# A planned kernel's order of instructions: a recorded list of 1677 search steps in place of 40 search rounds at build time

## The chip, the cores and the metric

The kernel runs on one core of one Trainium2 chip. The metric is the time of one execution in device microseconds. Before the change three runs were timed; their median stands below. One further execution was taken by the hardware profiler, and every view of the profile is of that one.

## The reference, cut to what matters

One inference step of a two-layer decoder in fp32, for a prompt of 512 tokens and a group of 8 x 8 sample tokens, which share all weights (576 tokens together; model width 1024, FFN width 2816):

```python
for i in range(DEPTH):                      # DEPTH = 2
    h = rms_norm(x, norm_mix_pre[i])
    if i % 2 == 0:
        m, nb = pool_mixer(h, ...)          # trailing means of 2, 4, 8, 16 tokens, a linear map per group
    else:
        m, nc, ns = gdn_mixer(h, ...)       # 8 q/k heads, 16 v heads of 128; chunked gated delta rule
    x = x + rms_norm(m, norm_mix_post[i])
    h = rms_norm(x, norm_ffn_pre[i])
    x = x + rms_norm(swiglu(h, ffn_w_in[i], ffn_w_out[i]), norm_ffn_post[i])
```

The outputs are x for both groups and the new states of the mixers.

## The kernel before, in words

Every product in fp32 accuracy is made from fp32r parts: an operand is split into a high and a low part (`wh`, `wl` for weights, `hH`, `hL` and `aH`, `aL` for activations), and `mm3` adds three matmuls per 128-row slice into one PSUM bank. ScalarE makes the high part, VectorE or GpSimd the low part. The 576 columns lie in two halves of 256 and 320 columns (`HALVES`); PSUM ring A of three banks serves the first half, ring B the second. In the DeltaNet layer other rings share the eight banks: `m` (two banks) for the projections, `s`, `k`, `x` and `g` for scan, inverse and transposes. Within the FFN a Strassen-like form (`seven`) is used. Weights arrive by SyncE's DMA queue in tiles of 128 x 1024 (`wraw`, three buffers) and are split as they come.

In time the work is: the pooling mixer, the first FFN, the projections and gates of the DeltaNet layer, its four groups of heads (`core`: inverse of the triangular matrices, scan over four chunks, sample heads) with the next group's projections, the output projection in two parts, and the second FFN. The first part of the output projection goes to DRAM (`y_d`); after the DeltaNet's tile pools are closed it is loaded again as `yo`, and the second part is added to it.

No engine's order is written by hand. The class `Plan` (from line 54) records every operation with its costs on each engine that may do it (`cost`), its predecessors, its shape mode on TensorE, and the PSUM tiles it holds. `finish` (line 267) then plans:

- `forward` (line 356) is a list scheduler. It walks through modelled time; on the engine that is free first it takes the ready operation with the highest `rank`. It models the DMA queue, the time of a change between TensorE's tile shapes, the TensorE clock by its load in a window, and the port that VectorE and GpSimd share. Operations marked for two engines (`EITHER`: VectorE or GpSimd; `BOTH`: VectorE or ScalarE) go to the one that takes them first. Where TensorE would wait over 300 ns in this model, `idle_until` puts dummy matmuls into an idle bank (`ps_w`, line 296; they compute nothing that is used). It returns the modelled length, the order and the times.
- `backward` (line 315) gives, for such an order, the latest time at which each operation could start. Its negative serves as the next rank.
- Before the change, `finish` made a first rank from the longest path, then 40 rounds: rank from `backward`, shifted per output tensor by a random amount of a width drawn from 0, 0, 300, 1000 and 3000 (modelled ns), then `forward`. A better round became the base of the next; the best of all was issued.

The instructions are issued in the order found, each engine's queue in strict order. All recorded operations therefore carry the line of that issue, L300, in the profile (dummies L296).

Of the kernel before, what the change touches and what calls it, by code (L numbers as in the profile page):

```python
# [4 lines left out]

# [45 lines left out]
ZB = (0, 4, 8, 10, 12, 16)  # L51


class Plan:


# [210 lines left out]
    def finish(self):  # L267
        self.on = False
        ops = self.ops
        n = len(ops)  # L270
# [4 lines left out]
        rank = [0.0] * n
        for i in range(n - 1, -1, -1):
            e = ops[i][7]
            hold, done = ops[i][1][e]
# [4 lines left out]
            rank[i] = r
        draw = random.Random(self.SEED)
        here = best = self.forward(rank)
        for _ in range(self.ROUNDS):
# [4 lines left out]
            if found[0] < best[0]:
                best = found
        with self.tc.manual_schedule():
            for i, e in best[1]:
                if e is None:
                    self.tc.nc.tensor.matmul(self.banks[i[0]][i[1]][0][:, :self.idle.shape[1]], self.idle, self.idle,  # L296
                                             start=True, stop=True)
# [2 lines left out]
                calls[e](*a, **k)  # L300

    def stirred(self, rank, stir, draw):

        if not stir:
            return rank
        off = {}
        for o in self.ops:
            off.setdefault(self.name(o), stir * (2.0 * draw.random() - 1.0))
        return [r + off[self.name(o)] for r, o in zip(rank, self.ops)]
# [506 lines left out]

# [1131 lines left out]
```

## Time and profile before

| what | value |
|---|---|
| median of 3 runs (lowest, highest) | 1572.15 us (1570.51, 1574.17) |
| the profiled execution's own time | 1572.64 us |
| its span, first to last instruction | 1570.9 us |
| instructions | 30641 |
| mean granted TensorE clock | 0.991 |
| HBM read, written | 166.65 MB, 30.52 MB |
| mean DMA rate over the span | 126 GB/s |

How to read it: PE is TensorE's matmuls, PEld its weight loads, DVE is VectorE, ACT ScalarE, POOL GpSimd, SP the SyncE queue that issues the DMAs. A row of a group gives the line, engine, operation, output<-inputs by tile name with the shape, the count, then the busy time in us and the mean ns of one, then the idle time just before. A row of the timeline gives the start and the length in us; in brackets stands the idle time before it and what ended that. In the windows view a row is one stretch: its length, then each engine's busy time with its count of instructions, the granted TensorE clock, the mean share of the DMA engines and GB/s. Matmuls are pipelined: several that overlap count once in the busy time.

### The profile page before, as it was taken

The page shows a single profiled execution, that of the slowest core. Times are in us where ns is not written, and L with a number is a line of the kernel's source. Part 1 is how long each engine was busy: PE and PEld are TensorE (multiplying, and loading weights), DVE is VectorE, ACT ScalarE, POOL GpSimd, SP SyncE. Part 2 cuts the span into 40 slices and gives each one's busy share as a digit, 9 for nine tenths or more (in the row PEclk, how much of TensorE's full clock was granted, in tenths as well). Part 3 has the DMA queues.
Part 4 walks back from the last instruction along what each step waited for, and adds up shares of the span by engine and source line. Part 5 has one row for each costly group of instructions (what it writes and reads, how often), then busy time and mean ns, then how long its engine had stood idle before and what let it go on. Part 6 is the DMA issues. An engine that isn't in the chain of part 4 may idle for free. (4 is left out here: it accounts for less than half of the span.)

```text
span 1570.9 us, 30641 instructions
## 1 busy us (share of the span) xinstructions
PE 1542.9 (98%) x11962; PEld 1481.2 (94%) x11962; DVE 1154.5 (73%) x2333; ACT 841.1 (54%) x1756; POOL 113.1 (7%) x258
## 2 busy tenths in 40 slices
...
PEclk8999999999999999999999999999999999999999
...
GB/s 184 103 178 142 82 94 95 96 80 91 151 210 158 83 119 117 102 123 100 136 109 108 106 127 120 201 140 179 248 173 177 107 81 73 88 110 68 98 187 119
DMA packets 350359, 198.92 MB, mean 127 GB/s; under 512 B 13963, under 2 KB 344364, under 8 KB 350207
## 3 DMA queue, kind: packets, MB, share of 16 engines
...
q14 instruction: 50, 0.41, 0.1%
HBM read 166.65 MB, written 30.52 MB: 126 GB/s over the span
## 5 line engine op out<-in xcount | busy, mean ns | idle before, releaser
L300 ACT ACTIVATE wh<-wraw 128x1024 fp32r<-128x1024 f32 (+1 forms) x227 | 233.5, 1032 | 263.2 <-PE ps_B L300 94.4
L300 DVE TENSOR_TENSOR wl<-wraw,wh 128x1024 fp32r<-128x1024 f32 (+2 forms) x226 | 268.0, 1191 | 113.6 <-ACT wh L300 74.9
L300 PE MATMUL ps_m<-hH,wh 128*128 128x320 f32 (+1 forms) x832 | 244.1, 310 | 2.7 <-ACT zz L300 2.6
L300 PE MATMUL ps_m<-hL,wh 128*128 128x320 f32 (+1 forms) x832 | 242.4, 306 | 0.0
L300 PE MATMUL ps_m<-hH,wl 128*128 128x320 f32 (+1 forms) x832 | 239.2, 306 | 0.0
L300 PEld LDWEIGHTS ps_m<-hH,wh 128*128 128x128 f32 x832 | 153.3, 189 | 7.6 <-ACT zz L300 3.6
L300 PEld LDWEIGHTS ps_m<-hL,wh 128*128 128x128 f32 x832 | 154.0, 190 | 2.3 <-issue 0.6
L300 PEld LDWEIGHTS ps_m<-hH,wl 128*128 128x128 f32 x832 | 152.6, 190 | 2.8 <-issue 0.8
L300 PE MATMUL ps_B<-hH,wh 128*128 128x320 f32 (+1 forms) x392 | 115.8, 306 | 0.2
L300 PE MATMUL ps_B<-hH,wl 128*128 128x320 f32 (+1 forms) x392 | 115.0, 305 | 0.0
L300 PE MATMUL ps_B<-hL,wh 128*128 128x320 f32 (+1 forms) x392 | 114.6, 304 | 0.0
L300 PE MATMUL ps_A<-hH,wh 128*128 128x256 f32 (+1 forms) x376 | 106.0, 293 | 2.8 <-DVE yo L300 1.9
L300 PE MATMUL ps_A<-hH,wl 128*128 128x256 f32 (+1 forms) x376 | 105.6, 292 | 0.5 <-DVE wl L300 0.5
L300 PE MATMUL ps_A<-hL,wh 128*128 128x256 f32 (+1 forms) x376 | 104.5, 290 | 0.1
L300 PE MATMUL ps_B<-aH,wl 128*128 128x320 f32 x352 | 103.5, 312 | 0.2 <-DVE wl L300 0.2
L300 PE MATMUL ps_B<-aH,wh 128*128 128x320 f32 x352 | 102.4, 311 | 0.0
L300 PE MATMUL ps_B<-aL,wh 128*128 128x320 f32 x352 | 101.9, 310 | 0.0
L300 PE MATMUL ps_A<-aH,wh 128*128 128x256 f32 x352 | 95.1, 283 | 0.4 <-ACT wh L300 0.4
L300 PE MATMUL ps_A<-aL,wh 128*128 128x256 f32 x352 | 94.0, 281 | 0.0
L300 PE MATMUL ps_A<-aH,wl 128*128 128x256 f32 x352 | 92.9, 282 | 0.0
L300 DVE SCALAR_TENSOR_TENSOR ac<-u,cwt,ac 128x600 f32<-128x600 f32 x96 | 80.9, 850 | 1.9 <-ACT ac L300 1.7
L300 ACT ACTIVATE aH<-sg 128x576 fp32r<-128x576 f32 (+2 forms) x56 | 32.3, 581 | 84.7 <-DVE sg L300 84.7
...
## 6 DMA issues: line engine op xcount, KB each, us to landing
...
```

The costliest lines, as they stand in the source:

```text
L300: calls[e](*a, **k)
```

## The change

`ROUNDS`, `STIR`, `SEED`, the random draws and `stirred` go. A string `MOVES` of 1677 entries comes, each of five numbers in base 36: `again.seed.stir.lo.hi`. `finish` starts from the same first rank and applies them in turn. An entry whose first field is 1 (16 of them, ten at the head of the list) replaces the rank by the backward pass of a forward pass. An entry with a width `stir` then adds to the rank of the operations lo to hi - 1 a noise of that width, which a hash makes from the seed and from the number of the first operation that writes the same tensor, so that operations that fill one tensor move together. The widths are 100 (550 entries), 300 (499), 1000 (363), 3000 (254) and 0 (11). Most ranges span 400, 100 or 1500 operations (573, 447 and 372 entries), a few the whole list; the highest bound is 15384. No order is compared with another any more: one last forward pass gives the order that is issued. `cost`, `forward`, `backward`, the operations and their data are unchanged.

```diff
+MOVES = """
+1.1eas61x.2s.4js.4mk 1.b5wlw6.2s.0.3q1 1.ktpsok.0.8pv.8sn 1.1ure0dv.0.5jj.6p7 1.hgmh6k.8c.981.bvc 1.7nyzhf.0.0.bvc
...
+"""
...
-    ROUNDS, STIR, SEED = 40, (0.0, 0.0, 300.0, 1000.0, 3000.0), 2
...
-        draw = random.Random(self.SEED)
-        here = best = self.forward(rank)
-        for _ in range(self.ROUNDS):
-            late = self.backward(here[1], here[2])
-            found = self.forward(self.stirred([-t for t in late], draw.choice(self.STIR), draw))
-            if found[0] < here[0] or draw.random() < 0.1:
-                here = found
-            if found[0] < best[0]:
-                best = found
+        first = {}
+        of = [first.setdefault(self.name(o), i) for i, o in enumerate(ops)]
+        for move in MOVES.split():
+            again, seed, stir, lo, hi = (int(x, 36) for x in move.split("."))
+            if again:
+                rank = [-t for t in self.backward(*self.forward(rank)[1:])]
+            if stir:
+                for i in range(lo, hi):
+                    rank[i] += stir * self.noise(seed, of[i])
+        best = self.forward(rank)
         with self.tc.manual_schedule():
...
+    @staticmethod
+    def noise(seed, who):
+
+        h = seed ^ (who * 2654435761 & 0xffffffff)
+        h ^= h >> 16
+        h = h * 0x85ebca6b & 0xffffffff
+        h ^= h >> 13
+        h = h * 0xc2b2ae35 & 0xffffffff
+        h ^= h >> 16
+        return h / 2147483648.0 - 1.0
```

More of the change, by code (lines that the diff above doesn't have):

```diff
@@ L2 @@
 import heapq
-import random
 from contextlib import ExitStack
@@ new lines @@
+0.yzlrz0.2s.0.s8 0.8bsca3.2s.2au.3gi 0.pd5qwx.8c.1zs.35g 0.1dkcr1g.2s.46o.49g 0.gohce9.8c.8hh.8k9
+0.1qmox10.2bc.7y1.895 0.1q0ubx9.8c.30w.3c0 0.2t46nq.8c.123.1d7 0.1f02old.2s.4cp.4nt 0.7uf57y.2s.383.3j7
+0.1io2edi.8c.6n2.6y6 0.d51t3g.8c.3ab.3lf 0.kyski6.2s.bg7.brb 0.nwmwau.8c.5ct.5fl 0.5q7dse.2bc.6gs.6jk
+0.94x3jt.2bc.52k.5do 0.173ehem.2s.3d.65 0.17dm05h.2s.1ar.2gf 0.7o5v0r.2s.a5c.bvc 0.19kwyb0.8c.5qe.5t6
+0.8fkj3m.2s.915.a6t 0.1gm8lpy.2s.4bn.5hb 0.gseya0.2bc.1jr.2pf 0.hb806i.rs.553.5g7 0.13th0bt.rs.bk1.bv5
@@ new lines @@
+0.xire0f.rs.1wy.32m 0.1wjfc1e.2s.9nf.at3 0.5mangj.rs.7re.7u6 0.1xbgl15.rs.7rh.82l 0.13tvkzy.rs.amh.axl
+0.ngzet1.rs.7wq.87u 0.1gjwecl.rs.2fc.2i4 0.xyipxv.8c.3ba.3me 0.12nn3ct.8c.2oc.3u0 0.3f9jym.2s.8d3.8fv
+0.ms49lm.8c.16t.2ch 0.10t15hv.8c.4zi.656 0.x1uzs9.2bc.9ni.9qa 0.1ipkmmg.2s.8oy.902 0.1du3687.rs.6vq.6yi
+0.7x2jcw.2s.aax.bgl 0.gu97up.8c.0.76 0.1hxvrax.8c.9q4.avs 0.y21u0p.2s.5fw.5r0 0.2bbt96.2bc.7ts.84w
+0.yldecn.2bc.11b.1cf 0.1tpg0gw.8c.1k3.1v7 0.rw51dw.8c.58h.6e5 0.8bcpst.rs.98t.aeh 0.7wpeg2.8c.8ql.91p
@@ new lines @@
+0.1y9p531.rs.3dl.3gd 0.m4xezo.8c.95k.ab8 0.1gj3768.2s.hn.1nb 0.51qq2b.2bc.2j6.2ly 0.1k3nqyr.2s.5lv.6rj
+0.y6ucev.rs.7z0.8a4 0.wxbkvk.2bc.7s3.837 0.1baxiw5.2s.0.kx 0.1q32nai.2s.70r.86f 0.1h4y1oy.2s.8jk.9p8
+0.1ttntui.8c.8c6.8na 0.1sdrihh.2bc.83k.86c 0.fun4eh.8c.bn5.bvc 0.1qmi15h.2s.0.t4 0.1o1of45.2s.618.76w
+0.1hdgjk2.rs.4mj.4pb 0.omnp9u.rs.6ox.6rp 0.1sta659.rs.5fw.5r0 0.fm47zb.8c.237.38v 0.v8iq9s.2s.73x.89l
+0.18l101a.2s.57e.92a 0.1ac1io.8c.7u7.8zv 0.1gvwjwn.2s.1xz.33n 0.1fxjl6j.2s.0.33f 0.5ez5wd.8c.3y8.49c
@@ new lines @@
+0.c9qi10.rs.azi.bam 0.ukl6ns.8c.7m6.7xa 0.141w03z.2s.9za.aae 0.4xpjy3.rs.7w2.876 0.wys13.2s.9u1.a55
+0.iwwn7d.8c.6xu.83i 0.hmfcbd.2bc.5cr.5fj 0.11wfrkv.rs.1fo.1qs 0.yc4sup.2s.77a.8cy 0.156z55c.rs.6p4.708
+0.wc5cgv.2s.6dr.6ov 0.kebtqw.8c.7be.7e6 0.1ui5xrl.2s.5p.40l 0.1kyvof3.8c.1hk.2n8 0.catp73.2bc.28f.2jj
+0.idq53h.8c.9j2.bvc 0.13d7t0r.8c.bbs.bmw 0.196fy4l.2s.2z4.44s 0.1jy9dbc.2s.6k1.6mt 0.hjty3u.2s.98l.ae9
+0.15bi1vd.8c.95m.bvc 0.1yyy23b.rs.1kd.1n5 0.167ecek.8c.9rt.a2x 0.idlzw1.2s.71u.awq 0.1sy5idv.rs.2i3.2kv
@@ new lines @@
+0.19s07wq.2bc.are.au6 0.5wbkzi.2s.8e3.9jr 0.30oiia.2bc.9hs.ang 0.ubjoux.2bc.96f.997 0.1idrsdh.2s.0.4f
+0.1345wfi.2bc.nw.z0 0.wl96k.rs.9fv.9qz 0.vts7qb.2bc.627.64z 0.1t5gy1n.rs.6xq.78u 0.1sz6l76.8c.24s.2fw
+0.1fpap5d.rs.1az.1dr 0.1nvzim1.2bc.734.7e8 0.1m0xezo.2s.sl.13p 0.are7a6.2s.94n.bvc 0.1bwzuvd.2s.9cy.bvc
+0.1ooajyd.8c.8b.b3 0.1tqhmtx.8c.abk.amo 0.15out6y.rs.87e.8a6 0.jfbmgm.8c.a0b.b5z 0.14knpgj.8c.71p.74h
+0.1omft1l.8c.8kg.8n8 0.14vl6lp.8c.bka.bvc 0.8dwfv7.rs.bp6.bry 0.45f1pl.8c.7qa.81e 0.1ya6poi.2bc.6xa.702
@@ new lines @@
+0.118i2z5.8c.bgv.bjn 0.1t08ub8.2s.3go.3rs 0.1u95a51.8c.az2.ba6 0.10a5k41.2s.a3y.af2 0.1jrwuu0.rs.6r0.724
+0.qcrc0f.2s.83u.8ey 0.3ee7l8.rs.584.6ds 0.xduik2.2bc.ajm.auq 0.ntzjlm.8c.7vz.7yr 0.1s5snnz.8c.bbh.be9
+0.16bi7kd.2bc.7ny.7z2 0.oyr52j.2bc.9ir.9tv 0.t8mqa1.2bc.a8r.ajv 0.nyhopk.2bc.bkp.bnh 0.1f9tfsk.8c.atg.bvc
+0.bxbllj.2s.74p.8ad 0.1h5gx65.2bc.5yf.617 0.y9gvui.2bc.8nu.8qm 0.7qssrm.rs.5um.65q 0.1okcgda.2s.brq.bvc
+0.k6xucp.2bc.aah.all 0.1wfieip.8c.ah2.bvc 0.d2ahld.2s.9zs.b5g 0.18rsote.8c.8oh.8r9 0.16t07f5.8c.7mj.7xn
@@ new lines @@
+0.tk1otn.8c.6cb.6nf 0.wu07gj.2bc.9k2.9mu 0.13jhfg3.rs.bpu.bvc 0.x5iue7.2bc.9hy.9kq 0.ulpwd0.2s.6qo.71s
+0.ukaov5.8c.5nv.5yz 0.s1yokp.2s.64c.7a0 0.xtalsn.2bc.63u.6ey 0.1co87nr.8c.gq.ru 0.14gv5nx.2s.9um.b0a
+0.2pclli.rs.434.45w 0.1074ifl.2s.b22.bvc 0.c16n9j.rs.7jx.7mp 0.1jwe87y.2s.bjn.bvc 0.waqa9f.8c.20a.35y
+0.1hkcexa.2s.6o5.6z9 0.z298wq.8c.5cx.5fp 0.cgt8km.2s.9ym.a9q 0.1qr6w9o.2s.a1h.bvc 0.1drnbq7.2s.423.7wz
+0.b3812m.8c.agu.ary 0.gtzd1n.2s.0.1fr 0.3u3inf.rs.255.27x 0.13mlg2v.2bc.b84.baw 0.1pemts2.8c.8cy.9im
@@ new lines @@
+0.frjlsp.rs.aia.ate 0.1ngbix6.2s.6hz.6t3 0.mzf1lv.2s.7t.1dh 0.1ftmuak.2s.94i.bvc 0.1fyuvqa.8c.1lp.2rd
+0.pweeor.2s.n2.1sq 0.1c29saf.2s.295.3et 0.bu9z7i.8c.236.2ea 0.u6ovvy.8c.1i2.2nq 0.14w485t.8c.1d9.1od
+0.9h9cjb.rs.4s2.4uu 0.39ebrs.8c.bpd.bs5 0.1am9j7r.rs.4kh.4n9 0.uhpayb.8c.ack.afc 0.11pmjpo.2bc.14f.2a3
+0.skurc5.2bc.4p2.4ru 0.1vnpwp2.2bc.4qj.51n 0.1rqy6x0.2s.0.qv 0.1bra9sb.8c.ajq.bvc 0.f61y4f.8c.5mo.5xs
+0.e17bj8.2s.89u.8ky 0.13vzi52.2bc.a52.a7u 0.ut9rpc.2s.0.1pz 0.ks5afa.2s.13v.1ez 0.ka59rm.2s.a09.a31
@@ new lines @@
+0.eq1qxn.2s.adp.aot 0.1n6fqsm.2s.3e0.78w 0.gagqcg.2bc.415.4c9 0.18apz9g.8c.71n.7cr 0.irgfs6.8c.a7b.aa3
+0.3hu8xb.8c.8p2.bvc 0.1t16y56.rs.4cm.4nq 0.1sh4e6b.2s.0.uu 0.hyn8m7.rs.5eo.5hg 0.1ha6ycs.rs.9pj.av7
+0.1bnmp46.2s.92q.9du 0.p365zt.2s.332.3e6 0.slrsm4.rs.2w1.2yt 0.12cd48q.8c.ako.bqc 0.1hbkupt.8c.a5w.ah0
+0.1894b8z.2s.5bi.6h6 0.1r7y4rp.8c.76l.7hp 0.1yzvtp6.2s.avd.bvc 0.hmp23.2s.4xc.630 0.1gwlwbr.rs.4an.4lr
+0.19m76dv.2s.5c1.5n5 0.1b5reu8.2s.2xz.43n 0.1k4pwt4.2s.343.49r 0.f4p0rd.2s.1aa.556 0.shjevs.2s.b2m.bvc
@@ new lines @@
+0.3uylj6.2s.9zl.aap 0.8qt0pb.8c.7k2.7mu 0.giv5rs.2bc.1pv.1sn 0.1n5q3ag.8c.aae.bg2 0.eiytoe.2s.3ky.4qm
+0.1n4p2wj.2s.0.qu 0.m9zqgh.2s.94o.bvc 0.doqgbu.8c.28h.3e5 0.16ydwyw.rs.bnu.bvc 0.1ntrap0.8c.8r9.92d
+0.nojzjm.rs.9ad.9lh 0.1erd6ij.rs.40b.433 0.1n4vgj6.8c.2wf.37j 0.1mluj8w.rs.bc7.bez 0.1kh0axy.8c.9ar.agf
+0.1eh5s7e.2bc.bql.bvc 0.9cgo5x.2s.adg.ag8 0.v5rr9k.8c.90u.a6i 0.1ntwdeu.rs.j3.u7 0.1ggkc0p.rs.4jd.4m5
+0.1c4rxlu.8c.45j.48b 0.16iwgxm.2s.87v.9dj 0.gfqtop.rs.1z8.2ac 0.oaccyp.2s.alw.brk 0.1n12t1d.rs.apy.b12
@@ new lines @@
+0.qxpuaj.2s.8sk.9y8 0.119oyih.2s.1x8.32w 0.vgqjdu.2s.85h.8gl 0.de4gjf.8c.2x5.389 0.n8ykow.2s.7qi.ble
+0.1my507t.rs.2vx.2yp 0.2afkkz.2s.9r7.awv 0.kijpe8.2bc.2cw.2o0 0.1qad7rx.rs.bb5.bm9 0.bxw1gm.2s.7s4.8xs
+0.l27x9p.rs.9c4.9n8 0.1v5i3um.rs.4ca.4f2 0.142ey1x.8c.a62.ah6 0.77r9sc.8c.8xo.90g 0.18u8v29.8c.8j1.9op
+0.1xbkpy.2bc.950.9g4 0.n9a5o9.rs.bh0.bs4 0.1rcffur.8c.2bl.3h9 0.brw6o2.rs.399.3kd 0.5ifxh1.2s.9w6.b1u
+0.1xwqwpr.2s.6yh.79l 0.skqprn.8c.bcy.bo2 0.fiuoy7.2s.1o9.1r1 0.4oo473.rs.7w6.87a 0.1dgs785.2s.b6x.bvc
@@ new lines @@
+0.1e63yrd.2s.mn.1sb 0.4s9imm.8c.bcg.bvc 0.1dv74ib.rs.95u.98m 0.12l74mb.rs.95f.987 0.kwhx1l.2s.3hm.4na
+0.1y9ermk.rs.9sa.9v2 0.1esb217.8c.wq.zi 0.1eipos.2s.4x9.62x 0.g53wqt.2s.2lj.3r7 0.1e06lim.rs.p5.1ut
+0.y2jd86.2bc.7ux.861 0.4w8lpx.2s.ar9.b2d 0.c5tmig.2s.8xw.990 0.5zg7at.rs.153.1g7 0.1tkh1py.8c.2lw.2x0
+0.sgy3db.rs.5pb.60f 0.78zd0w.8c.bk7.bvc 0.qt6hu0.rs.8lv.8wz 0.6rg9z2.8c.bka.bvc 0.1iwbcj5.2s.3a2.4fq
+0.1kmp8av.8c.an3.ay7 0.1q6ag36.2bc.7sn.83r 0.2er5z9.rs.7qw.7to 0.ellwxn.rs.2ti.2wa 0.xpz43v.8c.5rm.62q
@@ new lines @@
+0.19xn10y.rs.bn6.bvc 0.1aq0uo6.8c.8ro.92s 0.b09qp7.2s.5o2.5qu 0.whftwx.2bc.8uy.8xq 0.1bxgs3m.8c.4ni.5t6
+0.a814k4.8c.64i.6fm 0.wcz3tp.2bc.t0.144 0.1mkv1k1.2bc.43y.46q 0.uwtg4v.2s.uv.15z 0.jsmh9h.2s.cz.1in
+0.1ux0hk9.rs.9b2.9du 0.25r0dr.2s.3n6.3py 0.p218e9.rs.7jp.7mh 0.1cnf6tc.rs.5xe.606 0.1dhhtuv.rs.7y6.89a
+0.1j7t469.rs.8yf.917 0.10gcb38.2s.9a7.bvc 0.denvur.rs.as0.b34 0.n5xp1u.rs.b85.bvc 0.qd9vb6.rs.35h.389
+0.1nahjuq.2s.713.7c7 0.17hbpxi.8c.of.r7 0.yralpu.2bc.4fs.4qw 0.iupwe.2s.23i.5ye 0.6djjew.rs.9t7.9vz
@@ new lines @@
+0.g9cwui.2bc.1b7.1dz 0.42gz8r.8c.5xv.68z 0.1jvpfj2.rs.zb.123 0.7pjieu.2bc.88n.8bf 0.agcp8b.2bc.ajq.ami
+0.uyi5a5.8c.4nq.5te 0.1ek9jcd.rs.3qv.3tn 0.729suu.rs.5bg.6h4 0.1pmtgto.2s.812.8c6 0.pn7yi3.2s.7he.8n2
+0.1viijjt.2s.7wl.87p 0.g95tob.8c.1gr.1rv 0.g4u3my.rs.a3i.a6a 0.h1i307.2s.7jd.7uh 0.19er4xm.2bc.79v.7kz
+0.10ijetp.8c.3nz.3qr 0.hs9ns5.8c.1av.1lz 0.wzc8k9.8c.1lr.1wv 0.1lcw38t.rs.7dn.7or 0.mlg4th.2s.1e5.2jt
+0.12rz6ib.rs.b9.md 0.r3t49.2s.2pu.3vi 0.1s4x05a.2s.2u2.6oy 0.6db7f1.rs.5o3.5qv 0.1149pzm.rs.5jn.5mf
@@ new lines @@
+0.1yogjpm.2bc.7s6.7uy 0.1uvtod3.2s.1vl.319 0.14v01o0.rs.7wr.7zj 0.sgwwsd.8c.81t.84l 0.16ib8sw.rs.agn.ajf
+0.1pdldfo.rs.mh.p9 0.2bu01n.2bc.bfp.bih 0.1nkzscz.2s.ab1.bvc 0.qdl9r0.2s.b1g.bvc 0.1rb9urp.2s.25a.3ay
+0.x5ky0z.2s.2w2.376 0.8k12b5.rs.3ru.3um 0.pg2y4o.2s.329.47x 0.bmvqim.8c.84h.879 0.a0kqqh.rs.bif.bvc
+0.1ysljy9.2s.3ee.3pi 0.g6hzq1.2s.5c2.6hq 0.x0i0jp.8c.a54.ag8 0.mqa5a1.2s.5md.5xh 0.h1h51v.rs.abf.amj
+0.1jn9f00.8c.7jt.7ux 0.pco7fb.2s.0.qd 0.1o79yfh.2s.3dq.3ou 0.9p57i3.2bc.2k2.2mu 0.137oyfy.2bc.244.2f8
@@ new lines @@
+0.1df7pw8.8c.0.1i8 0.1dyuhzc.2s.bfm.bie 0.i7st28.2s.5gg.5rk 0.1fsdiiv.8c.5ol.6u9 0.zz50ro.2s.4j8.4uc
+0.1xumun6.8c.3d3.3fv 0.19hvl8t.8c.9sp.a3t 0.1iub5qn.2s.j2.1oq 0.1unem5p.2bc.4s5.539 0.v1o74t.2s.3hc.4n0
+0.1xns34g.8c.0.1kr 0.l2km10.8c.1jo.1us 0.1r3ol8u.rs.9sh.9v9 0.1a2446a.8c.ad.1g1 0.k529el.2s.all.br9 0.rf4z3g.2s.gp.1md
+0.1oyuzv6.2s.az8.bvc 0.5lpl4g.8c.8qz.923 0.clofeh.2bc.66o.6hs 0.2qv9ve.2s.3ee.3h6 0.1aeqiu8.2s.7rm.bmi
+0.5ve8qy.8c.0.uw 0.i2zoje.2s.0.1pd 0.1n6b1pl.2s.9v3.b0r 0.1575h9a.2s.a15.ac9 0.zh71ty.2bc.4q4.4sw 0.vrt1ug.2s.b1d.bch
@@ new lines @@
+0.1er3avv.2s.9g0.bvc 0.u67jbk.8c.aed.ah5 0.uggpa7.2s.b1c.bvc 0.r862q2.8c.5l6.5ny 0.1rwvw1a.8c.3fy.3r2
+0.1cbr4ph.2s.afg.aqk 0.19sm67d.2bc.5yg.69k 0.gt8d8h.8c.8ku.9qi 0.fl6vs3.8c.5q.8i 0.b8gkdk.8c.9p4.aus
+0.11ulhk0.8c.47s.4iw 0.qz3oe1.rs.7e3.7p7 0.695vu6.2s.14a.29y 0.czx0jw.rs.9q6.a1a 0.1m16ygq.rs.bgn.bjf
+0.1hq38i6.2bc.54e.576 0.10dfl84.rs.2gn.2rr 0.9qymy8.2s.0.xe 0.4kaai7.2s.awd.bvc 0.1i65yu4.8c.9s8.9v0
+0.16kbm7y.rs.ac8.af0 0.414xty.2bc.sx.vp 0.10ada2e.2s.4ir.4tv 0.r9hw6e.2s.a20.bvc 0.n6wrie.2s.8ig.8tk
@@ new lines @@
+0.ur5ltm.2s.vv.21j 0.qxwa4z.rs.9l4.9w8 0.12nicjl.2s.jt.1ph 0.kdzszn.8c.b4a.bfe 0.1nsa3q7.8c.5zd.751
+0.8fgxcc.2s.9ua.bvc 0.wif3o0.2s.axz.bvc 0.kairnz.8c.bc8.bnc 0.xhduts.2bc.btk.bvc 0.3mmv8r.8c.0.q7
+0.198au1n.2bc.4cu.4fm 0.1px3ics.2bc.13p.1et 0.1i3pmnp.2bc.4vo.4yg 0.1nn7j0f.2s.185.1j9 0.1bj6h0v.8c.9w2.bvc
+0.up39z0.rs.bfd.bi5 0.1tati4g.2s.0.1bn 0.1dymz3h.2bc.437.45z 0.vubpsz.8c.b0v.bbz 0.hq2cnj.rs.2g2.2iu
+0.oq4kod.2bc.9p3.9rv 0.qqjmz4.2s.9z1.a1t 0.ojzbv5.2s.2qd.3w1 0.1dcfpcj.2s.9fu.ali 0.92wz18.2bc.1kp.1nh
```

245 lines of the change are left out of this document (238 added, 7 removed).

## The prediction

> **What bounds the kernel now.** I read the head of the page first, then a table of seven stages. The stages are the start and pooling mixer (0 to 120 us), the first FFN, the turn into the gated-DeltaNet layer, that layer, its seam with the output projection, the second FFN, and the end. The first three lines are of the page, the others of the windows view.
>
> ```profile
> span 1570.9 us, 30641 instructions
> PE 1542.9 (98%) x11962; PEld 1481.2 (94%) x11962; DVE 1154.5 (73%) x2333; ACT 841.1 (54%) x1756; POOL 113.1 (7%) x258
> PEclk8999999999999999999999999999999999999999
> ```
> ```profile
> 0.00:120.00 120.00, 113.99 (x780) 107.80 (x781) 93.87 (x220) 77.83 (x166) 30.06 (x88) 0.91 0.54 155
> 120.00:460.00 340.00, 339.42 (x2525) 337.67 (x2524) 221.04 (x332) 139.05 (x209) 3.20 (x4) 1.00 0.38 111
> 460.00:600.00 140.00, 136.27 (x989) 129.33 (x988) 115.39 (x282) 92.37 (x199) 15.36 (x35) 0.99 0.48 135
> 600.00:1000.00 400.00, 392.57 (x3431) 357.94 (x3430) 339.58 (x857) 266.49 (x697) 51.30 (x117) 1.00 0.41 116
> 1000.00:1190.00 190.00, 185.73 (x1447) 176.36 (x1444) 129.80 (x264) 97.53 (x226) 13.17 (x14) 1.00 0.63 187
> 1190.00:1530.00 340.00, 340.00 (x2525) 339.14 (x2523) 231.43 (x343) 144.17 (x217) 0.00 (x0) 1.00 0.37 109
> 1530.00:1571.00 41.00, 34.93 (x284) 33.01 (x282) 23.36 (x40) 23.66 (x46) 0.00 (x0) 0.94 0.35 114
> ```
>
> After the length come PE, PEld, DVE, ACT and POOL, then the clock. PE is the bound everywhere: it is idle for 1570.9 - 1542.9 = 28.0 us. The two FFN stages, 680 us together, leave 0.6 us of idle: no order can shorten them. What an order can change lies in the other 890 us.
>
> PE's busy time is not all work. The planner puts dummy matmuls (ps_w, line 296) where its own clock sees PE wait for over 300 ns. The windows view of this tile alone says where:
>
> ```profile
> 0.00:120.00 120.00, 6.13 (x34) 5.41 (x34) 0.91 0.54 155
> 460.00:600.00 140.00, 4.73 (x34) 4.14 (x34) 0.99 0.48 135
> 600.00:1000.00 400.00, 1.71 (x10) 1.43 (x10) 1.00 0.41 116
> 1000.00:1190.00 190.00, 9.57 (x80) 9.29 (x80) 1.00 0.63 187
> 1530.00:1571.00 41.00, 1.28 (x10) 1.20 (x10) 0.94 0.35 114
> sum 1571.00, PE 23.41 PEld 21.46; mean PE 3.34 PEld 3.07
> ```
>
> So 168 dummies cover 23.4 us of waiting that the plan knows of. The timeline shows the first run of them, the largest one with what ends it, and PE's last work:
>
> ```profile
> 1.27 2.93 PE L296 MATMUL ps_w<-ones 128*128 128x128 f32 x12 [1.27 <-POOL ones L92]
> 1092.33 2.01 ACT L300 ACTIVATE wh<-wraw 128x1024 fp32r<-128x1024 f32 x2 [2.57 <-DMA og<-og_d]
> 1094.72 6.86 PE L296 MATMUL ps_w<-ones 128*128 128x128 f32 x60
> 1097.08 0.89 DVE L300 TENSOR_TENSOR hL<-og,hH 128x320 fp32r<-128x320 f32 x2
> 1097.66 6.54 SPq L300 DMA_DIRECT2D yo<-y_d  x11
> 1102.90 1.14 DVE L300 TENSOR_TENSOR yo<-yo,ps_A 128x256 f32<-128x256 f32 x3 [4.93 <-issue]
> 1103.47 0.36 PE L300 MATMUL ps_A<-hH,wh 128*128 128x256 f32 x1 [1.89 <-DVE yo L300]
> 1564.03 1.58 PE L300 MATMUL ps_B<-ident,gy 128*128 128x128 f32 x7
> ```
>
> The seam at 1094.72 is one hole of 8.75 us (to 1103.47). A reload of yo may only start when the closed pools' last reader (hL) is done. It is issued at 1097.66, its first sum is at 1102.90, and only that sum frees a PSUM bank.
>
> **The change, part by part.** The work is the same: every matmul, activation and DMA stays, only its place in its queue (and, for operations that two engines can do, its engine) changes, so no term is an added instruction. The 1677 steps run while the program is built and cost the chip nothing. SP's queue is reordered with the rest, loads before stores or behind them, and POOL's (113 us busy) takes more or fewer operations off DVE; both count only where PE then waits, and no row of before tells which way they go. What can move is PE's waiting. I sum it against the profiled execution, 1572.64 us, whose span is 1570.9; the runs' median of 1572.15 is 0.5 below it.
>
> Known holes. Dummies without the first run, which waits for the first constants and inputs: 23.4 - 2.9 = 20.5 us. Bounds of the gain: 0 (each hole is a chain of data) and 20.5. In the largest, 1102.90 - 1097.66 = 5.2 us are the reload, which no order shortens. The other 8.75 - 5.2 = 3.5 us, 40%, hang on how early hL is made and how much PE work is kept back. Before it ACT waited 2.57 us for a load of og, a thing of SP's order. With work kept back, some of the 5.2 can be covered too. I take half: 10.2 us.
>
> Other waits. Idle 28.0, less 1.3 at the start and less the tail after PE's last matmul, 1570.9 - 1565.6 = 5.3: 21.4 us. Who ended them, by PE's view of waits:
>
> ```profile
> PE ps_m L300 <- ACT zz L300: 2.6, 4, 1.0
> PE ps_A L300 <- DVE xst L300: 2.1, 1, 2.1
> PE ps_A L300 <- DVE yo L300: 1.9, 1, 1.9
> PE ps_x L300 <- DVE vt L300: 1.6, 4, 0.6
> PE ps_k L300 <- DVE ks L300: 1.5, 3, 0.6
> ```
>
> They are many and short; no single one is over 2.1 us. The plan covers nothing under 300 ns, and where its costs are off it does not see the wait at all. In the DeltaNet stage PE is idle for 400 - 392.6 = 7.4 us while dummies fill only 1.7. Bounds: a loss as large as the term (below, a rival) and 21.4. A search can lower only those that its model has, so I take 0.3 of it: 6.4 us.
>
> Stalls inside busy time. A row of matmuls counts as busy when one starts late by less than its modelled length. The timeline at the start of an inverse, and the prices of two forms:
>
> ```profile
> 607.77 0.42 PE L300 MATMUL ps_m<-hL,wh 128*128 128x256 f32 x2
> 608.33 0.30 PE L300 MATMUL ps_k<-T,Uw 128*64 128x32 f32 x2
> 608.56 0.41 PE L300 MATMUL ps_m<-hH,wl 128*128 128x320 f32 x1
> 609.15 1.07 PE L300 MATMUL ps_k<-T,Uw 128*64 128x32 f32 x30 [0.18 <-ACT wh L300]
> ```
> ```profile
> L300 PE MATMUL ps_m<-hH,wh 128*128 128x320 f32 (+1 forms) x832 | 244.1, 310 | 2.7 <-ACT zz L300 2.6
> L300 PEld LDWEIGHTS ps_m<-hL,wh 128*128 128x128 f32 x832 | 154.0, 190 | 2.3 <-issue 0.6
> L300 PE MATMUL ps_k<-S,qk 128*128 128x256 f32 x96 | 26.6, 384 | 0.3 <-DVE sn L300 0.2
> ```
>
> Between the starts 607.77 and 608.33 lie two matmuls, and none of it is idle. A change of tile shape (128*128 to 128*64) stands there, and the second one comes 0.59 us after the single matmul at 608.56, of which 0.18 is idle. Fewer changes between shapes is what a better order can bring. The weight loads bound it: from 460 to 1190 us PEld is not busy for 10.7 + 42.1 + 13.6 = 66.4 us, and PE for 3.7 + 7.4 + 4.3 = 15.4, so 51 us are neither. Most of that is no stall: the fp32 matmuls (ps_k<-S,qk, 384 ns) outlast their 190 ns loads whatever the order. Bounds: a loss of a few us from more turns, and 51. I take 2 us, near nothing, since the row that shows one shows 0.2 to 0.4 us each.
>
> The Trainium skill, in "Trainium Kernel Development and Optimization" under "Best Practices", holds that LDWEIGHTS busy share, not matmul busy share, measures the distance to the roofline. Here the one is 94%, the other 98%. By that rule the reserve is 1570.9 - 1481.2 = 89.7 us and half of it would give 1528; I do not go by it, for the fp32 matmuls named.
>
> Clock. The granted clock is 0.91 over the first 120 us, 0.99 over 140, 0.94 over the last 41: 10.8 + 1.4 + 2.5 = 14.7 us of full clock lost, most of it at the start and the last after PE's end. Bounds: a loss of the same kind, if a new hole is not covered, and 12. I take 1.5. The skill's "TensorE: Matmul & The Clock Gate", under "What's actually happening", says that the activity window is free-running and does not restart with the kernel. By it, which hole costs half clock would be chance, and this term 0; the rows of one execution cannot show that.
>
> Sum: 10.2 + 6.4 + 2 + 1.5 = 20.1 us. 1572.6 - 20.1 = 1552.5 on the profiled execution's scale, 1552 on the median's. If the cover of the known holes goes (dummies left out where the chip still waits), their own time turns into idle and nothing is lost; where a wait goes, the next matmul group is limited by its own start-to-start pitch.
>
> **Rivals.** The larger gain: the search closes nearly all known holes (say 18 of 20.5), half of the other waits (10.7), and thins the turns (8): 37 us, 1535. For it: 1677 steps against 40 tries, and local ones. Against: the chains of data, of which the seam's reload alone is 5.2.
>
> The smaller gain: the plan's holes move rather than close, as each is a chain. Of the seam go the 3.5 us, of the rest a quarter of 12: 6.5 us, 1566.
>
> No change: the plan's own gain lies in what the chip does not share. Only the seam's 3.5 us fall and as many are lost in new short waits: 1572.
>
> Slower. A tighter plan leaves less slack before every group. The place is the DeltaNet stage, where DVE is busy for 339.6 of 400 us and feeds wl, and ACT empties the two banks of ps_m. The 832 ps_m matmuls of one kind are 104 groups of eight, and one waited up to 1.0 us (ACT zz). If each starts 0.3 us late, because queues in strict order pass on what the plan's costs miss, that is 31 us against the 20.1 gained: 1583. It decides from 20.1 / 104 = 0.19 us a group. Against it: now only 4 such waits are seen, 2.6 us in all.
>
> Not what it says: the steps name ranges of operations by number. If they were made for another list, they would be noise, and the last order is taken without comparing it to others as before, so it would be some per cent slower. Against: their highest bound is 15384, the size of this kernel's list (the page counts 16,309 instructions of PE, DVE, ACT and POOL, dummies and set-up among them). I give it 0.02 within "slower".
>
> **How the numbers follow.** Forecast (a gain of 12 to 28 us) 0.50, larger gain 0.18, smaller 0.14, no change 0.07, slower 0.11. 0.2% is 3.1 us, about what a measurement of this kernel tells from none. Faster: 0.50 + 0.18 + 0.14 = 0.82; same 0.07; slower 0.11. The range leaves out slower and no change, 0.18, and a gain beyond the larger rival, about 0.02: from 1534 to 1569. The forecast's own range is 1544 to 1560.
>
> **What would show it.** In the changed kernel the FFN stages keep some 2525 matmuls in 340 us at full busy. The count of ps_w falls from 168 to about 80 to 110, and the run of 60 at the seam to 20 to 45, with the hole there 4 to 6 us. The sum of PE's waits falls from 21 to about 15 us, and PE busy from 1542.9 to some 1529. The layers begin earlier by a few us each: the second FFN at about 1171 in place of 1190. It is wrong if the dummies fall and idle rises by as much (the plan's gain is not the chip's), if ps_m's idle row grows from 2.7 to over 20 us (the slower rival), or if PE's busy time falls by over 30 us (turns were worth more).

## The result and the profile after

| | median of runs (lowest, highest) | ratio to before, 95% interval |
|---|---|---|
| before | 1573.16 us (1570.51, 1575.55; 4 runs) | 1 |
| after | 1552.41 us (1549.25, 1553.56; 4 runs) | 0.9865 [0.9842, 0.9888] |

The change makes the kernel 20.7 us, 1.35%, faster. The profiled execution of after took 1553.56 us, with a mean granted clock of 0.997 (before 0.991). The head of its page:

```profile
span 1551.9 us, 30356 instructions
PE 1524.7 (98%) x11852; PEld 1463.7 (94%) x11852; DVE 1157.1 (75%) x2311; ACT 837.2 (54%) x1766; POOL 116.6 (8%) x268
PEclk9999999999999999999999999999999999999999
```

The shares say nothing: PE is 98% busy before and after. One has to subtract. The span fell by 19.0 us. PE's idle time is 1551.9 - 1524.7 = 27.2 us against 28.0, so 0.8 of the 19.0 is idle and 18.2 is busy time. The windows view of after's dummies (ps_w) alone says how much of that was dummies; the columns are length, PE, PEld, clock, DMA share, GB/s:

```profile
0.00:120.00 120.00, 8.03 (x44) 7.01 (x44) 0.97 0.54 155
460.00:600.00 140.00, 0.00 (x0) 0.00 (x0) 1.00 0.49 138
600.00:1000.00 400.00, 0.00 (x0) 0.00 (x0) 1.00 0.42 119
1000.00:1190.00 190.00, 0.69 (x4) 0.53 (x4) 1.00 0.66 195
1190.00:1530.00 340.00, 1.28 (x10) 1.20 (x10) 1.00 0.37 108
sum 1571.00, PE 10.00 PEld 8.73; mean PE 1.43 PEld 1.25
```

Dummies went from 168 and 23.4 us to 58 and 10.0 us: 13.4 of the 19.0. The remaining 18.2 - 13.4 = 4.8 us are matmuls of the same work that show less busy time, late starts hidden in it among them. Next the windows view of all engines, in the stages of the prediction:

```profile
0.00:120.00 120.00, 115.04 (x807) 109.65 (x808) 98.82 (x224) 78.90 (x168) 26.75 (x86) 0.97 0.54 155
120.00:460.00 340.00, 339.56 (x2518) 337.00 (x2517) 222.52 (x336) 138.68 (x211) 3.60 (x4) 1.00 0.39 112
460.00:600.00 140.00, 137.87 (x1016) 131.36 (x1015) 119.55 (x291) 91.23 (x200) 18.42 (x38) 1.00 0.49 138
600.00:1000.00 400.00, 387.15 (x3437) 352.89 (x3436) 333.88 (x823) 270.33 (x717) 53.63 (x124) 1.00 0.42 119
1000.00:1190.00 190.00, 189.15 (x1416) 180.47 (x1415) 140.64 (x280) 99.53 (x224) 14.20 (x17) 1.00 0.66 195
1190.00:1530.00 340.00, 339.54 (x2537) 336.79 (x2536) 231.20 (x341) 150.04 (x232) 0.00 (x0) 1.00 0.37 108
```

The first FFN is as it was, and the seam stage (1000 to 1190) is nearly full. One line is worse: in the DeltaNet stage PE is idle for 400 - 387.15 = 12.85 us, where it was 7.4. PE's view of waits names what grew:

```profile
PE ps_x L632 <- DVE vt L632: 4.0, 7, 1.4
PE ps_A L632 <- DVE xst L632: 2.1, 1, 2.1
PE ps_m L632 <- ACT u L632: 1.7, 2, 0.9
PE ps_k L632 <- DVE QD L632: 1.6, 4, 0.5
PE ps_k L632 <- ACT sn L632: 1.5, 1, 1.5
```

The wait for `vt` rose from 1.6 to 4.0 us, those for `QD` and `sn` are new at the top, and the two for `zz` and `yo` are gone. Stages shift, so here is also the start of the same matmul in each trace (us; the last column is the best kernel of the experiments, m3 below):

| PE starts | before | after | m3 |
|---|---|---|---|
| one matmul within the first FFN (`ps_B<-tH,th`) | 161.1 | 162.0 (+0.9) | 157.8 (-3.3) |
| last matmul of the first FFN's output | 469.9 | 469.6 (-0.3) | 463.8 (-6.1) |
| inverse of the first group of heads | 608.3 | 602.5 (-5.8) | 596.7 (-11.6) |
| inverse of the fourth group | 989.0 | 983.7 (-5.3) | 971.6 (-17.4) |
| fourth ps_A group of the second output part | 1103.5 | 1085.6 (-17.9) | 1070.0 (-33.5) |
| last matmul | 1565.3 | 1546.5 (-18.9) | 1529.7 (-35.6) |

The start of one matmul also moves when the order around it changes, so these rows show that the gain comes in the turn and at the seam, but not how much each gave. A count of all work shows that better. Each operation of the plan was matched with its matmuls in the trace, and the modelled time of all operations started so far, without dummies, was compared. By this count after is ahead of before by 1.5 us at 460 us of before's time, 10.9 at 560, 8.2 at 1080, 17.8 at 1110 and 19.0 at the end. So the turn gave 9.4 us, the DeltaNet groups lost 2.7, and the seam gave 9.6. The windows agree: without dummies, after has started 10 matmuls more than before by 460 us, 71 by 600, 87 by 1000 and 132 by 1190.

These rows show the seam, the first of before's timeline, the others of after's:

```profile
1084.58 0.28 PE L300 MATMUL ps_A<-hH,wh 128*128 128x256 f32 x1
```
```profile
1073.73 0.28 PE L632 MATMUL ps_A<-hH,wh 128*128 128x256 f32 x1
1080.39 1.88 SPq L632 DMA_DIRECT2D yo<-y_d  x4
1084.69 0.42 DVE L632 TENSOR_TENSOR yo<-yo,ps_A 128x256 f32<-128x256 f32 x1 [0.98 <-DMA yo<-y_d]
```

PE can fill three banks of ring A before the first sum frees one. In before the first of those three groups started at 1084.58, all three were through when the dummies began at 1094.72, and the first sum came at 1102.90, 18.3 us after the first start: hence the hole. In after it comes 1084.69 - 1073.73 = 11.0 us after: the reload is issued 6.7 us behind the first group and not 13.1, and itself takes 4.3 us and not 5.2. The last projections and scan steps run among the three groups, so no hole is left. PE over those 10 us, in the windows view (85 matmuls, none idle):

```profile
1080.00:1090.00 10.00, 10.00 (x85) 1.00 0.77 223
```

### The profile page after: what moved, and what is told of

Its sections match the earlier page's. It is cut to its first block, busy times and chain, and to the rows that moved or that the text cites. A ratio compares the mean times of both kernels' runs of the same rounds, so it can differ in the third digit from the quotient of the medians.

```text
span 1551.9 us, 30356 instructions
## 1 busy us (share of the span) xinstructions
PE 1524.7 (98%) x11852; PEld 1463.7 (94%) x11852; DVE 1157.1 (75%) x2311; ACT 837.2 (54%) x1766; POOL 116.6 (8%) x268
## 4 chain that ended last, share of the span: by engine, by line
PE 41%; DVE 9%; DMA 2%; ACT 2%; issue 1%; DVEq 0%; ACTq 0%; SPq 0%
PE ps_B L632 15%; PE ps_A L632 12%; PE ps_m L632 7%; PE ps_s L632 3%; PE ps_k L632 2%; DVE ac L632 2%; DVE ii L632 1%; PE ps_x L632 1%; DVE wl L632 1%; DVE vt L632 1%; DMA wraw<-in_ffn_w_in_dram 1%; DMA QD<-c_d 1%; PE ps_n L632 0%; DMA vt<-z_d 0%; DMA out_dram<-St 0%
## 5 line engine op out<-in xcount | busy, mean ns | idle before, releaser
L632 PE MATMUL ps_m<-hH,wh 128*128 128x320 f32 (+1 forms) x832 | 248.8, 312 | 1.7 <-ACT u L632 1.7
L632 PE MATMUL ps_m<-hL,wh 128*128 128x320 f32 (+1 forms) x832 | 245.6, 306 | 0.0
L632 PE MATMUL ps_m<-hH,wl 128*128 128x320 f32 (+1 forms) x832 | 244.7, 307 | 0.0
L632 PEld LDWEIGHTS ps_B<-hH,wh 128*128 128x128 f32 x392 | 72.8, 188 | 1.3 <-ACT wh L632 0.6
```

## The experiments

The plan has a length of its own, the time that its model gives the order. It is a number of the planner, no time of the chip: 1530.3 us before, 1496.0 after. The plan thus promised 34.3 us, and the chip gave 20.7. Two questions followed: what of the prediction's reasons for the gain holds, and where the other 13.6 us stayed. For the second I aligned each operation's start on the chip with its modelled start. The chip lags behind the plan by 9.8 us at 560 us and 36.8 at 1080 in before, by 13.4 and 48.0 in after. Some 7 and 9 us of it arise in the first 160 us, and in each FFN the lag grows by 1 to 4 us. So most of what is lost is lost in the DeltaNet layer, and in that alignment some two thirds of this sit where PE goes from a projection matmul to a small fp32 one of scan or inverse: 17.0 us over 232 such places in before, 25.4 over 264 in after (the expectation of e3 below has 19.0 and 23.7 for them).

**Dummies left out (e1, e2).** The prediction held that cover costs nothing if it goes. The two dummy matmul lines were taken out of each kernel, so their work, which nothing uses, is not done:

```diff
                 if e is None:
-                    self.tc.nc.tensor.matmul(self.banks[i[0]][i[1]][0][:, :self.idle.shape[1]], self.idle, self.idle,
-                                             start=True, stop=True)
                     continue
```

> The kernel before with its order unchanged and all dummy matmuls (84 operations, 168 records) left out; they compute nothing that is used. Theory (a dummy only fills a wait): the holes stay as idle, the time is 1573 within 3 us, PE idle grows from 28 to about 50 us. Rival (the dummies hold the granted clock): after the holes at 544 and 1094 us the clock halves for one to three windows of 3.4 us, each costing 1.7 us of matmul time, and the start, which has 32 of them, loses more: 1578 to 1590, mean clock below 0.985.

> The changed kernel with its order unchanged and its 29 dummy operations (58 records) left out. Theory: 1552 within 3 us, since only the start and the end have any. Rival (clock): the start loses what the changed kernel had won there (clock 0.97 over the first 120 us in place of 0.91), 1556 to 1562.

Measured: before without dummies 1582.84 us, 1.0043 [1.003, 1.0056]; after without dummies 1556.86 us, 0.9893 [0.9871, 0.9915] against after's 0.9865 [0.9842, 0.9888]. The windows of e1, first start, then turn and seam:

```profile
0.00:120.00 120.00, 107.46 (x710) 101.11 (x710) 90.29 (x211) 74.64 (x161) 28.83 (x88) 0.90 0.51 145
460.00:600.00 140.00, 132.74 (x929) 125.78 (x928) 113.78 (x263) 93.73 (x201) 18.86 (x39) 0.95 0.47 131
1000.00:1190.00 190.00, 177.47 (x1430) 168.47 (x1427) 123.42 (x248) 99.34 (x233) 9.96 (x12) 0.97 0.64 188
```

Where the dummies stood in the large holes the clock falls from 0.99 to 0.95 and from 1.00 to 0.97. That is 0.04 x 140 + 0.03 x 190 = 11 us of full clock in this execution, which at 1586.82 us is the longest of ten; by the ratio all runs lose 6.8 us, by the medians 8.7. In the ten executions the mean clock is 0.983 to 0.989, in those of before beside them 0.991 to 0.996, so the loss comes each time. So the dummies do hold the clock, and a hole without cover costs more than its own length. In after they still seem to be worth some 0.3%, but the intervals overlap. Both times came out as the rival of the expectation had them, not its theory.

**A price for the detour (e3, e4).** One theory of the lag was a hidden price, about 0.085 us, each time PE leaves an fp32r product for an fp32 matmul and returns. Into after's FFN stages, where PE is full, 466 fp32 dummy operations were set one at a time, or 468 in runs of four, between the matmuls of one product, writing idle banks that nothing reads:

```diff
-            for i, e in best[1]:
+            for i, e in self.detours(best[1], 4, 1):
...
+                        if seen % every == 1:
+                            for b in (6, 7):
...
+                                    out += [((b, turn[b]), None)] * run
```

e4 calls it with 16, 4: one run of four at every sixteenth place.

> The changed kernel with 466 extra dummy fp32 matmuls into a bank that is idle, one at a time, each between two fp32r matmuls of one group in the two FFN stages, where PE is never idle. A dummy's own pitch is 2 records of 0.111 us, so 466 are 103 us. Theory (leaving a run of fp32r matmuls and coming back costs about 0.085 us beside the work, as the 232 and 264 such detours of the DeltaNet stage slip by 19.0 and 23.7 us against the plan): 1552 + 103 + 40 = 1695. Rival (no such cost; the slip is waiting for operands): 1552 + 103 = 1655.

> The same number of extra dummies (468) at the same places, but four at a time, so 117 detours. Theory: 1552 + 104 + 10 = 1666, 29 us under the kernel with single ones. Rival (no cost for a detour): 1656, the same as the kernel with single ones within 3 us.

Measured: 1650.83 us, 1.0484 [1.0464, 1.0504], and 1654.08 us, 1.05 [1.048, 1.052]. Against after's ratio that is (1.0484 - 0.9865) x 1574.11 / 466 = 0.209 us for a lone operation and 0.0635 x 1574.11 / 468 = 0.214 for one of a run. With the price, e3's 349 more detours would have cost 30 us more than e4; it is 3 us faster. The theory falls. The groups of dummies in e3 and then e4 look as if it held:

```profile
L628 PE MATMUL ps_w<-ones 128*128 128x128 f32 x990 | 188.5, 275 | 1.3 <-POOL ones L423 1.3
```
```profile
L628 PE MATMUL ps_w<-ones 128*128 128x128 f32 x994 | 133.2, 277 | 1.3 <-POOL ones L423 1.3
```

Busy time is 188.5 against 133.2 us for the same number of matmuls of the same mean length. But overlapping records of one group count once, and those beside other matmuls do not overlap each other. Only the kernel's time decides.

**New order in one part (h1 to h4).** The old 40 rounds were kept to get the old ranks, and old and new ranks were joined by operation number, the new ones shifted by the median difference at the joint. For h4:

```diff
-        best = self.forward(rank)
+        best = self.forward(self.spliced(old, rank))
...
+        off, end = gap(6000), gap(10000)
+        return old[:6000] + [x + off for x in new[6000:10000]] + [x + off - end for x in old[10000:]]
```

h1 has new ranks below 7000 (through the turn), h2 from 9000 on (late DeltaNet, seam, second FFN), h3 below 6000 and from 10000 on, h4 between these alone (the middle of the DeltaNet layer).

> The kernel before's plan, with the new ranks for the operations up to number 7000 alone (start, first FFN, gates, the first DeltaNet group), shifted by one constant so that the two join. The plan's own length is 1513.3 us (before 1530.3, changed 1496.0). Theory (the gain is the closing of two holes, at the gates and at the seam): the gates' part, 8 us, and 2 to 3 at the start: 1563. Rival (the gain lies all over the list, 0.6 us for each planned us): 17.0 x 0.6 = 10 us, 1563 as well; the two differ below.

> The new ranks for the operations from number 9000 on alone (the last DeltaNet group, output projection, seam, second FFN). Plan's length 1517.4 us. Theory: the seam's 13 us: 1560. Rival (0.6 of 12.9): 1565.

> The new ranks up to number 6000 and from 10000 on, the old ones for the three middle DeltaNet groups between. Plan's length 1500.0 us. Theory: both holes close and the middle keeps the old order, whose short waits are the smaller: 1573 - 8 - 13 - 2 = 1550, as fast as the changed kernel or up to 5 us faster. Rival (0.6 of 30.3): 1555.

> The new ranks for the operations 6000 to 10000 alone (the middle DeltaNet groups), the old ones elsewhere. Plan's length 1530.2 us, as before. Theory: no hole of the plan is closed, so 1573 within 3 us. Rival (the new order of the middle is itself worse on the chip, since it waits there 2.3 us more): 1577 to 1582.

| kernel | plan, us | chip, us | ratio, 95% interval |
|---|---|---|---|
| h1, head new | 1513.3 | 1564.60 | 0.9938 [0.992, 0.9955] |
| h2, tail new | 1517.4 | 1567.34 | 0.9956 [0.9945, 0.9968] |
| h3, both ends new | 1500.0 | 1553.27 | 0.9866 [0.9847, 0.9885] |
| h4, middle new | 1530.2 | 1579.86 | 1.0034 [1.002, 1.0048] |

The head gives 9.8 us and the tail 6.9, of 17.0 and 12.9 in the plan; the 13 us expected of the tail were a miss. Counted by PE's work, h2 does gain 9.7 us at the seam, from 4.6 behind before at 1080 us to 5.1 ahead at 1110; it lost those 4.6 between 800 and 1000 us, in the later groups of heads. h3 is as fast as after with the old middle. h4 is the clear one: its plan is as long as before's, and the chip is 5 us slower. The page and the view of waits of h4 in the DeltaNet stage (PE 392.6 busy in before, 1.6 us in `vt`):

```profile
600.00:1000.00 400.00, 386.99 (x3353) 354.81 (x3353) 336.00 (x842) 264.79 (x704) 54.91 (x119) 1.00 0.41 115
```
```profile
PE ps_x L645 <- DVE vt L645: 5.6, 8, 1.3
```

The new order of the middle brings the waits of after's middle with it: 13 us idle and the one for `vt`. From h3 to after the plan gains 4.0 us and the chip nothing. In both settings the middle is worth 4 to 5 us less on the chip than in the plan. The search won modelled time there that the chip does not have.

**Why the model is off there (m1 to m4).** Two causes could be seen. Theory A: a cost is wrong. Behind many operations of ACT and DVE that write fewer than 128 partitions, the next one starts 0.11 to 0.13 us later than planned. In after's timeline of ACT (start, length):

```profile
615.26 1.21 ACT L632 ACTIVATE Uw<-ps_s 64x512 f32<-64x512 f32 x2 [1.39 <-PE ps_s L632]
616.50 0.33 ACT L632 ACTIVATE cstt<-ps_x 128x192 f32<-128x192 f32 x1
629.18 0.60 ACT L632 ACTIVATE kt<-ps_x 128x512 f32<-128x512 f32 x1
629.65 0.63 ACT L879 ACTIVATE ve<-ps_s,bkd 128x128 f32<-128x128 f32 x2
```

Two 64x512 evictions hold ACT for 616.50 - 615.26 = 1.24 us, 0.62 each; after a 128x512 of 0.60 the next starts 0.47 us later, before its end. DVE's rows:

```profile
622.22 0.61 DVE L632 SCALAR_TENSOR_TENSOR rs<-ps_k,ngc,vt 128x128 f32<-128x128 f32 x2
622.74 0.84 DVE L632 SCALAR_TENSOR_TENSOR ac<-u,cwt,ac 128x600 f32<-128x600 f32 x1
624.15 0.59 DVE L632 SCALAR_TENSOR_TENSOR sn<-ps_k,ngc,vs 64x128 f32<-64x128 f32 x2
624.77 0.43 DVE L632 TENSOR_TENSOR sn<-ps_k,gcq 64x256 f32<-64x256 f32 x1
```

The two of 128x128 take 0.61 us together, and the next row starts at 622.74, before their end at 622.83. The two of 64x128 take 0.59 us together and 0.33 each, so they overlap one another; the next row starts at 624.77, after their end at 624.74. The planner gives all of them the shorter, overlapped hold. The Trainium skill, in "ScalarE: Activation LUTs" under "What ACT_TABLE_LOAD costs", has back-to-back ACTIVATEs, measured on tiles of 128 partitions, overlap by some 93 ns; the row of 128x512 agrees with that (0.60 - 0.47 = 0.13 us), and the rows of 64x512 show that it does not hold for every pair.

The number of partitions is not what decides, though. Later in ACT's timeline a 64x512 eviction overlaps its successor like a wide one (0.48 us from start to start), and a 128x512 does not (0.62):

```profile
1516.79 0.58 ACT L632 ACTIVATE yT<-ps_A 64x512 f32<-64x512 f32 x1
1517.27 0.46 ACT L632 ACTIVATE nsq<-yo 128x320 f32<-128x320 f32 x1
```
```profile
637.94 0.60 ACT L632 ACTIVATE kt<-ps_x 128x512 f32<-128x512 f32 x1 [0.61 <-PE ps_x L632]
638.56 0.63 ACT L632 ACTIVATE qk<-ac 128x512 f32<-128x512 f32 x1
```

The kernel's operations show what differs: the partition at which an operand starts. Of the two evictions into `Uw` the first reads `ps_s` from partition 0 and the second from 64, and `cstt` reads from 0 again. The row at 624.77 reads and writes from 64, the two before it from 0. `qk` reads SBUF from 0, where ACT's last read of SBUF (`vs`) was from 64. `yT` and its neighbours all start at 0. Matched with the trace one by one, after's operations sort by this. Take the pairs that follow each other without a pause. Where the second one reads or writes SBUF or PSUM from another start partition than the last read or write there, none of 86 pairs on ACT and none of 151 on DVE overlap, and in 93 of these the first operation has all 128 partitions. Where nothing changes, 35 of 39 pairs on ACT and 46 of 48 on DVE overlap behind a narrow operation, by a median of 93 and 74 ns. So the number of partitions, which m2 below plans by, is a stand-in. It is right for 144 of the 231 pairs behind a narrow operation, and it misses the 93 behind a wide one.

Theory B: slack. An order in strict queues passes on every small delay, and a search against an exact clock removes the slack that takes them up.

So the recorded steps were followed by more of the same kind, each kept if the modelled length fell or grew by little (78 of m1's 167 steps lengthen its plan, by up to 0.22 us): m1 under unchanged costs (167 steps, a control for searching longer), m2 with narrow operations holding their engine for their whole length (232 steps), m4 with longer latencies between engines, 100 ns to PE and 60 ns to the others (237 steps), m3 with both, the latencies at 60 and 40 ns (260 steps). m3's edit; m2 lacks the LAT line, m4 the hold:

```diff
+        self.ops = [o[:1] + ({e: (h[1], h[1]) if e in ("ACT", "DVE") and self.parts(o) < P else h for e, h in o[1].items()},)
+                    + o[2:] for o in ops]
+        self.LAT = {e: t + {"PE": 60.0, "SP": 0.0}.get(e, 40.0) for e, t in self.LAT.items()}
+        for move in MORE.split():
+            _, seed, stir, lo, hi = (int(x, 36) for x in move.split("."))
+            for i in range(lo, hi):
+                rank[i] += stir * self.noise(seed, of[i])
         best = self.forward(rank)
```

> The changed kernel with 167 further accepted steps of the same kind, found under the plan's own unchanged costs. The plan's length falls from 1496.0 to 1495.4 us. A control for the three that follow. All theories: 1552 within 3 us; if another draw of steps alone moves the chip's time by more, the differences of the other three have to be read against that.

> The changed kernel, then one cost of the plan mended, then 232 steps found under the mended cost. The plan lets each ScalarE and VectorE operation overlap the next one on its engine by 0.10 or 0.085 us; in the traces those that write fewer than 128 partitions do not (pitch 0.11 to 0.13 us over the plan's, equal to their own length). Under the mended cost the changed kernel's ranks plan to 1509.3 us, the new ones to 1496.9. Theory A (the short waits that the plan does not foresee in the DeltaNet stage come from this cost): the chip takes over 0.6 of the 12.4 us, 1552 - 7 = 1545. Theory B (they come from tightness as such: any plan without slack pays them): 1552 within 3 us.

> As the one before, and beside it 0.06 us more from any producer to TensorE and 0.04 us more to the other engines, with 260 steps found under these costs (planned 1505.5 us, the changed kernel's ranks 1531.9). Theory A: no better than mended costs alone, 1545 to 1548, since the slack is paid for nothing. Theory B: the slack absorbs late operands, 1540 to 1546 and at least 4 us under mended costs alone.

> The changed kernel with the plan's costs as they are, but 0.10 us more from any producer to TensorE and 0.06 us more to the others, and 237 steps found under these (planned 1507.9 us, the changed kernel's ranks 1536.2). Theory A: about as the changed kernel, 1550 within 3. Theory B: 1540 to 1546.

| kernel | chip, us (lowest, highest) | ratio to before, 95% interval |
|---|---|---|
| m1, longer search | 1553.84 (1552.00, 1554.95) | 0.9869 [0.9844, 0.9894] |
| m2, mended costs | 1546.89 (1544.36, 1548.38) | 0.9822 [0.9797, 0.9847] |
| m4, slack | 1544.42 (1544.17, 1546.46) | 0.9813 [0.9789, 0.9838] |
| m3, both | 1539.79 (1536.42, 1541.28) | 0.9778 [0.9752, 0.9804] |

The control moves nothing. Mending the cost wins 7 us on it, slack alone 9, both together 14: each theory's edit pays, and together they pay more than either. (The intervals of m1 and m2 just touch, but the slowest run of m2 is 3.6 us under the fastest of m1.) Counted by PE's work, m2 is ahead of m1 by 1.4 us at 560 us and by 8.6 at 1080, so its gain comes in the DeltaNet layer, where Theory A puts it. m4 is ahead by 5.0 us already at 460 and by 7.8 at 1080; why slack pays so much before that layer was not looked into. m3 beats both kernels of this case, after by some 13 us. Its page and its windows of the turn and the DeltaNet stage:

```profile
span 1534.7 us, 30364 instructions
PE 1514.7 (99%) x11862; PEld 1459.3 (95%) x11862; DVE 1157.4 (75%) x2314; ACT 842.1 (55%) x1763; POOL 113.8 (7%) x265
```
```profile
460.00:600.00 140.00, 139.83 (x1091) 134.35 (x1091) 118.12 (x286) 96.64 (x206) 19.01 (x42) 1.00 0.49 136
600.00:1000.00 400.00, 394.02 (x3452) 359.27 (x3452) 338.33 (x836) 277.16 (x738) 49.85 (x119) 1.00 0.43 123
```
```profile
PE ps_x L695 <- DVE vt L695: 1.4, 3, 0.7
```

PE's idle time is 1534.7 - 1514.7 = 20.0 us against after's 27.2; in the DeltaNet stage it is 6.0 against 12.85 (m2 7.6, m4 9.4, m1 11.2), and the wait for `vt`, in the last of these lines, is back at 1.4. (It is 2.1 in the control m1, so it is no sign of either edit.) The dummies did not fall: 11.8 us against 10.0. By the table of starts m3 is ahead of after by 5.8 us at the end of the first FFN, 12.1 at the fourth inverse and 15.6 behind the seam. So some 5 us of its lead arise by the end of the first FFN, where after had gained little. The clock of the first 120 us is 1.00 in this execution, which is the fastest of four, 3.4 us under their median.

What stays open: how far m2's and m4's gains are their theories', and how far the luck of another order. Three other orders (after, h3, m1) lie within 1.5 us of each other, so luck of 7 us is unlikely, though h3 and m1 are close relatives of after. Each edit was run with one order only. That a change of the start partition ends the overlap was read in the traces; neither a kernel of its own nor a plan that goes by it was run.

## Why the prediction came out right

The predicted 1552 us and the measured 1552.41 agree, but the terms do not. Two errors cancel, so it is luck that the number is right to 0.4 us.

- Known holes: predicted 10.2 us, half of 20.5. Measured: dummies fell by 13.4 us, none of it in the first run, and the short idle pieces between dummies and the next matmul, which the sum had left under "other waits", by another 3. The term was too small by 3 us, by 6 with these pieces. What I missed is that two large holes were no fixed chains: the seam closed entirely (predicted 4 to 6 us left), since the reload's start, not its length, set most of it. That start does not hang on the last `hL` either, as the prediction had it: after issues the reload at 1080.39, while DVE's last `hL` starts at 1081.65. And the 34 dummies of the turn went because the gates' small steps (ps_g below, in PE's timeline) now lie among projections from 532 us on, where they had stood among dummies from 546.1 on (the first three lines are before's).

```profile
546.10 0.33 PE L300 MATMUL ps_g<-misc,t_gt 128*128 128x64 f32 x2
546.36 0.39 PE L300 MATMUL ps_g<-misc,s_gt 64*128 64x16 f32 x2
546.68 1.60 PE L296 MATMUL ps_w<-ones 128*128 128x128 f32 x12
```
```profile
532.04 0.30 PE L632 MATMUL ps_m<-hH,wl 128*128 128x320 f32 x1
532.18 0.33 PE L632 MATMUL ps_g<-misc,t_gt 128*128 128x64 f32 x2
532.32 0.39 PE L632 MATMUL ps_m<-hH,wh 128*128 128x320 f32 x1
```

- Other waits: predicted a gain of 6.4 us. Measured: idle time 28.0 to 27.2, and without the pieces at the dummies a loss of about 2, the DeltaNet stage's 5.4 among it. This step failed. It held that a search lowers the waits that its model has, and took 0.3 of the sum; h4 and m2 show that the search in this stage traded them against waits that the model lacks.
- Late starts and clock: predicted 2 + 1.5, together 3.5; measured 4.8 of busy time. The place was wrong in part: the clock of the first 120 us rose from 0.91 to 0.97, worth 7 us of full clock, but by the count of PE's work only 2.5 us of gain stood at 120 us and 1.5 at 460. Idle time and dummies together took 13.0 of the first 120 us, 12.1 in before. That changes of tile shape were the reason was not tried; e3 and e4 rule out a price for leaving fp32r products, not one for shapes.
- "If the cover of the known holes goes, nothing is lost" was wrong: e1 measured 0.43%.
- The slower rival named the right stage and the right kind of fault, short waits in the DeltaNet layer behind DVE and ACT. It missed tile and size: ps_m's idle row stayed small, the waits came at ps_x and ps_k, and h4 puts them at 5 us, not 31. "No change" had the reason for the missing 13.6 us: a part of the plan's gain lies in what the chip does not share.
- The signs named: the FFN stages kept 2518 and 2537 matmuls; ps_w fell to 58, below the 80 to 110; PE busy fell to 1524.7 where 1529 was expected; PE's waits did not fall to 15 us; the run of 60 at the seam fell to 4, not to 20 to 45; a matmul of the second FFN began 16.9 us earlier (1225.8 to 1208.9), where 19 was said.
- The Trainium skill's rule in "Trainium Kernel Development and Optimization", "Best Practices", that LDWEIGHTS busy share, not matmul busy share, shows the distance to the roofline, seems at first not to track this kernel: the span less PEld's busy time is 89.7 us before, 88.2 after and 75.4 in m3, while the span fell by 19.0 and 36.2. But PEld's busy time holds the dummies' loads too, 21.5, 8.7 and 10.2 us. Without them the distance is 111.2, 96.9 and 85.6 us, and it falls by some three quarters of what the span does.
